# Split GELU product: tiles 2 to 13 taken in pairs of 16 adjacent rows a partition, with joint stores and three rotating buffers

## The chip, the core and the metric

The kernel runs on one core of one Trainium2 chip. The metric is device time in microseconds (us) for one execution, as the median of several runs. A profile is one further execution, recorded by the hardware profiler; its times are counted from the start of its span.

## The reference

The input is `x` of shape 32 x 512 x 2048 in float32, that is 16,384 rows of 2048 values, 134.2 MB. The output has 1024 values for each row, 67.1 MB.

```python
x1, x2 = (x[..., :half_dim].copy(), x[..., half_dim:].copy())
gelu_x1 = 0.5 * x1 * (1 + erf(x1 / np.sqrt(2)))
return (gelu_x1 * x2).astype(np.float32)
```

Each row is read once, its first half goes through GELU, and the result is multiplied by its second half. No value is used twice.

## The kernel before

The rows are cut into 16 tiles of 1024 rows. In a tile, each of the 128 partitions holds R = 8 adjacent rows, so a load brings 64 KB of adjacent bytes to a partition (8.4 MB a tile), and a store writes 32 KB of adjacent bytes from it (4.2 MB a tile).

There are two `x` buffers and two `o` buffers, used by even and odd tiles in turn. A tile goes through four steps. Its load is issued by SyncE (SP) in `load` at L49. ScalarE (ACT) computes GELU from the first half of each row in `x` to `o` at L87, in steps of 5 and 3 rows; tiles 0 and 15 take steps of 2, 2 and 4 rows. VectorE (DVE) multiplies `o` in place by the second half of `x` at L95. A store takes `o` to HBM at L56. ScalarE issues the stores of tiles 0 to 13, and SyncE those of tiles 14 and 15. Tiles 0 and 15 are stored in two halves, tile 0 is also loaded in two halves, and a tiny load on ScalarE's queue comes first.

The order is written out by hand with semaphores. `gelu_done` counts the steps of ScalarE and releases VectorE. `mul_done` counts the multiplications; it releases each store on the queue that issues it, and on SyncE the load of tile i+2, which takes the `x` buffer of tile i. `ready[k]` counts both the loads into `x` buffer k and the stores out of `o` buffer k. ScalarE waits for it before the first step of a tile, so that it waits for the load of tile i and for the store of tile i-2 together:

```python
nc.scalar.wait_ge(ready[k], n[ready[k].name])
...
if i + 2 < n_tiles:
    nc.sync.wait_ge(mul_done, n[mul_done.name])
    load(i + 2, slice(0, R), ready[k])
```

Each engine works through its own instructions in order, waits included. The loads of tiles 0 and 1 are issued ahead of the loop.

Of the kernel before, what the change touches and what calls it, by code (L numbers as in the profile page):

```python
# [1 line left out]

# [4 lines left out]

GELU = mybir.ActivationFunctionType.Gelu


@with_exitstack
def kernel(
    ctx: ExitStack,
    tc: tile.TileContext,
    x: bass.AP,
    out: bass.AP,
):
    nc = tc.nc
    P = nc.NUM_PARTITIONS

    x_flat = x.flatten_outer_dims()
    out_flat = out.flatten_outer_dims()
    n_rows, dim = x_flat.shape
    half = dim // 2

    R = 8
    x_t = x_flat.rearrange("(n p r) d -> n p r d", p=P, r=R)
    o_t = out_flat.rearrange("(n p r) d -> n p r d", p=P, r=R)
    n_tiles = x_t.shape[0]
    x_bufs = [nc.alloc_sbuf_tensor(f"x{k}_tile", [P, R, dim], x.dtype) for k in range(2)]  # L30
    o_bufs = [nc.alloc_sbuf_tensor(f"o{k}_tile", [P, R, half], out.dtype) for k in range(2)]

    first = [nc.alloc_semaphore(f"first{j}") for j in range(2)]
    ready = [nc.alloc_semaphore(f"ready{k}") for k in range(2)]
    gelu_done = nc.alloc_semaphore("gelu_done")
    mul_done = nc.alloc_semaphore("mul_done")
    tail_stored = nc.alloc_semaphore("tail_stored")
    opened = nc.alloc_semaphore("opened")  # L40
    scrap = nc.alloc_sbuf_tensor("scrap_tile", [8, 128], x.dtype)
    n = {sem.name: 0 for sem in [*first, *ready, gelu_done, mul_done, tail_stored, opened]}

    def counted(ins, sem, by):
        ins.then_inc(sem, by)
        n[sem.name] += by

    def load(i, rows, sem):
        ins = nc.sync.dma_start(out=x_bufs[i % 2][:, rows, :], in_=x_t[i][:, rows, :])  # L49
        counted(ins, sem, 16)  # L50
        return ins

    def store(queue, i, rows, sem):
        queue.wait_ge(mul_done, n[mul_done.name])
        counted(
            queue.dma_start(out=o_t[i][:, rows, :], in_=o_bufs[i % 2][:, rows, :]), sem, 16  # L56
        )

    opening = nc.scalar.dma_start(out=scrap[:, :], in_=x_t[0][:8, 0, :128])
    counted(opening, opened, 16)
    for ins in (
        opening,
        load(0, slice(0, 4), first[0]),
        load(0, slice(4, 8), first[1]),
        load(1, slice(0, 8), ready[1]),
    ):  # L70
        tc.no_tile_sem_insts.add(ins.ins.name)
    tc.close()
    tc.compile()  # L73

    for i in range(n_tiles):
        k = i % 2
        last = i == n_tiles - 1
        pieces = i == 0 or last
        steps = ((0, 2), (2, 4), (4, 8)) if pieces else ((0, 5), (5, 8))
        for lo, hi in steps:  # L80
            rows = slice(lo, hi)
            if i == 0 and lo % 4 == 0:
                nc.scalar.wait_ge(first[lo // 4], 16)
            elif lo == 0:
                nc.scalar.wait_ge(ready[k], n[ready[k].name])
            counted(
                nc.scalar.activation(  # L87
                    out=o_bufs[k][:, rows, :], in_=x_bufs[k][:, rows, :half], func=GELU
                ),
                gelu_done,  # L90
                1,
            )
            nc.vector.wait_ge(gelu_done, n[gelu_done.name])
            counted(
                nc.vector.tensor_mul(  # L95
                    out=o_bufs[k][:, rows, :],
                    in0=o_bufs[k][:, rows, :],
                    in1=x_bufs[k][:, rows, half:],
                ),
                mul_done,  # L100
                1,
            )
            if pieces and hi % 4 == 0:
                if last:
                    store(nc.sync, i, slice(hi - 4, hi), tail_stored)
                else:
                    store(nc.scalar, i, slice(hi - 4, hi), ready[k])
        if not pieces:
            if i == n_tiles - 2:
                store(nc.sync, i, slice(0, R), tail_stored)  # L110
            else:
                store(nc.scalar, i, slice(0, R), ready[k])
        if i + 2 < n_tiles:
            nc.sync.wait_ge(mul_done, n[mul_done.name])
            load(i + 2, slice(0, R), ready[k])


    nc.scalar.wait_ge(opened, 16)
    nc.scalar.drain()  # L119
    for sem in (*first, *ready, opened):  # L120
        nc.scalar.sem_clear(sem)
    nc.vector.drain()
    nc.vector.sem_clear(gelu_done)
    nc.sync.sem_clear(mul_done)
    nc.sync.wait_ge(tail_stored, n[tail_stored.name]).then_inc(
        tail_stored, -n[tail_stored.name]
    )


# [1 line left out]
_INS = ['x']  # L131
_OUTS = [((32, 512, 1024), 'float32')]


# [23 lines left out]
```

## Time and profile before

| what | value |
|---|---|
| time, median of 3 runs | 469.36 us (469.31 to 469.44) |
| span of the profiled execution | 467.84 us |
| median time less that span | 1.52 us |
| bytes moved over the span | 201.34 MB, mean 430 GB/s |
| VectorE busy | 140.5 us in 34 instructions |
| ScalarE busy | 115.5 us in 35 instructions |
| loads, issue to landing, median | 44.4 us (15 of the 17) |
| stores of 4 MB on ScalarE's queue, issue to landing, median | 44.7 us |

The span is the time from the first to the last record of the profiled execution. Queue q1 in the profile carries the DMAs that SyncE issues, and queue q10 those that ScalarE issues. Both run on the core's 16 DMA engines. A DMA of 128 partitions is split over all 16 engines, so that each of them moves 8 partitions, in 8 packets. The share of a queue is the time that its packets took, as a part of the time of 16 engines. A name such as `ACTq L56` is a DMA issue on ScalarE's queue at line 56. A "landing" is the moment at which the whole DMA has counted up its semaphore.

### The profile page before, as it was taken

How to read it: one execution, taken by the hardware profiler on the slowest of the kernel's cores; microseconds unless marked ns; L12 is line 12 of the kernel's file. 1: busy time of each engine (PE TensorE's matmuls, PEld its weight loads, DVE VectorE, ACT ScalarE, POOL GpSimd, SP SyncE). 2: the span in 40 equal slices, each digit the busy share in tenths (PEclk: the TensorE clock that was granted, in tenths of full speed). 3: DMA queues.
4: the chain of work that ended last, by engine and by line, in shares of the span. 5: the costliest groups of instructions: out<-in, count | busy, mean ns of one | idle time of the engine just before them, and what ended most of it. 6: DMA issues, size and time to landing. Idle time of an engine off the chain costs nothing.

```text
span 467.8 us, 154 instructions
## 1 busy us (share of the span) xinstructions
DVE 140.5 (30%) x34; ACT 115.5 (25%) x35; POOL 0.2 (0%) x4
## 2 busy tenths in 40 slices
DVE  0330515207051060511606115060150702507043
ACT  1320606041060410604105050050501506014060
POOL 0000000000000000000000000000000000000000
DMA  8999999999999999999999999999999999999988
GB/s 359 448 448 448 398 406 496 403 403 448 459 437 403 440 412 493 403 403 448 487 409 403 445 406 493 403 403 448 493 403 403 448 426 471 403 426 426 493 384 379
DMA packets 5057, 201.34 MB, mean 430 GB/s; under 512 B 568, under 2 KB 576, under 8 KB 576
## 3 DMA queue, kind: packets, MB, share of 16 engines
q1 hardware_dynamic: 2880, 142.61, 70.6%
q10 hardware_dynamic: 2176, 58.73, 29.1%
q14 instruction: 1, 0.01, 0.0%
HBM read 134.22 MB, written 67.11 MB: 430 GB/s over the span
## 4 chain that ended last, share of the span: by engine, by line
DMA 76%; DVE 14%; ACT 8%; ACTq 0%; SPq 0%; issue 0%
DMA out_dram<-o_tile 66%; DVE o_tile L95 14%; DMA x_tile<-in_x_dram 10%; ACT o_tile L87 8%; ACTq L119 0%; SPq L49 0%
## 5 line engine op out<-in xcount | busy, mean ns | idle before, releaser
L95 DVE TENSOR_TENSOR o_tile<-o_tile,x_tile 128x5120 f32<-128x5120 f32 (+3 forms) x34 | 140.5, 4171 | 319.7 <-ACT o_tile L87 319.7
L87 ACT ACTIVATE o_tile<-x_tile 128x5120 f32<-128x5120 f32 (+3 forms) x34 | 114.3, 3407 | 337.3 <-DMA out_dram<-o_tile 301.8
L87 ACT ACT_TABLE_LOAD x1 | 1.3, 1283 | 2.9 <-PEq L73 2.9
L142 POOL MEMSET const-bfloat16-1.0<- 128x1 bf16 x1 | 0.1, 102 | 0.0
L142 POOL MEMSET const-uint8-127<- 128x1 uint8 x1 | 0.1, 101 | 0.0
L142 POOL MEMSET const-float32-0.0<- 128x1 f32 x1 | 0.1, 99 | 0.2 <-issue 0.2
L142 POOL MEMSET const-float32-1.0<- 128x1 f32 x1 | 0.1, 98 | 0.0
## 6 DMA issues: line engine op xcount, KB each, us to landing
out_dram<-o_tile ACTq DMA_DIRECT2D x13, 4096.0 KB, 44.7
x_tile<-in_x_dram SPq DMA_DIRECT2D x2, 4096.0 KB, 16.7
out_dram<-o_tile ACTq DMA_DIRECT2D x2, 2048.0 KB, 34.4
out_dram<-o_tile SPq DMA_DIRECT2D x1, 4096.0 KB, 25.2
out_dram<-o_tile SPq DMA_DIRECT2D x2, 2048.0 KB, 7.8
x_tile<-in_x_dram SPq DMA_DIRECT2D x15, 44.4
scrap_tile<-in_x_dram ACTq DMA_DIRECT2D x1, 4.0 KB
```

The lines of the kernel that those rows point to most:

```text
L87: nc.scalar.activation(out=o_bufs[k][:, rows, :], in_=x_bufs[k][:, rows, :half], func=GELU),
L95: nc.vector.tensor_mul(out=o_bufs[k][:, rows, :], in0=o_bufs[k][:, rows, :], in1=x_bufs[k][:, rows, half:],),
L142: nc = _bacc.Bacc("TRN2", target_bir_lowering=False, num_devices=1)
```

## The change

Tiles 2 to 13 (`PAIRED`) are taken in pairs of an even and an odd tile. In a pair, partition p holds 16 adjacent rows of the 2048-row block: the first 8 belong to the even tile, the other 8 to the odd one. Each tile is still loaded by one DMA with 64 KB of adjacent bytes for each partition, but the partitions are now 128 KB apart in HBM instead of 64 KB.

The `x` and `o` buffers are replaced by three buffers of 64 KB a partition, each of which holds one loaded tile. Odd tiles use buffer 1, and even tiles use buffers 0 and 2 in turn (`buf_of`). GELU now works in place, on the first half of each row. The multiplication writes its products, packed, into the buffer of the even tile: the even tile's products to its lower half, the odd tile's to its upper half (`out_rows`). When the odd tile is multiplied, one store of 64 KB a partition takes both tiles to HBM (`store_pair`, 8.4 MB). Tiles 0, 1, 14 and 15 keep their rows and their separate stores.

The loads of tiles 0, 1 and 2 are issued ahead of the loop. After that, loads are issued at odd tiles only: SyncE waits for the multiplication of tile i, issues the load of tile i+2 into buffer 1, then waits for the store of the pair to land, and issues the load of tile i+3 into the buffer from which that store has read. VectorE waits for its own previous multiplication before each new one. The instructions of ScalarE and VectorE keep their number and the elements they work on. The stores of tiles 2 to 13 are six DMAs instead of twelve.

```diff
-    x_bufs = [nc.alloc_sbuf_tensor(f"x{k}_tile", [P, R, dim], x.dtype) for k in range(2)]
-    o_bufs = [nc.alloc_sbuf_tensor(f"o{k}_tile", [P, R, half], out.dtype) for k in range(2)]
+    n_tiles = n_rows // (P * R)
+    PAIRED = range(2, n_tiles - 2)
 
+    def rows_of(flat, i):
+        if i in PAIRED:
+            first = (i - i % 2) * P * R
+            block = flat[first : first + 2 * P * R, :]
+            return block.rearrange("(p r) d -> p r d", p=P)[:, (i % 2) * R : (i % 2 + 1) * R, :]
+        return flat[i * P * R : (i + 1) * P * R, :].rearrange("(p r) d -> p r d", p=P)
 
+    bufs = [nc.alloc_sbuf_tensor(f"m{k}_tile", [P, 2 * R, half], x.dtype) for k in range(3)]
+
+    def buf_of(i):
+        return 1 if i % 2 else i % 4
+
+    def x_rows(i, lo, hi, part):
+        pairs = bufs[buf_of(i)][:, 2 * lo : 2 * hi, :].rearrange("p (r two) d -> p r two d", two=2)
+        return pairs[:, :, part, :]
+
+    def out_rows(i, lo, hi):
+        at = (i % 2) * R
+        return bufs[buf_of(i - i % 2)][:, at + lo : at + hi, :]
...
-    def load(i, rows, sem):
-        ins = nc.sync.dma_start(out=x_bufs[i % 2][:, rows, :], in_=x_t[i][:, rows, :])
+    def load(i, lo, hi, sem):
+        pairs = bufs[buf_of(i)][:, 2 * lo : 2 * hi, :].rearrange("p (r two) d -> p r (two d)", two=2)
+        ins = nc.sync.dma_start(out=pairs, in_=rows_of(x_flat, i)[:, lo:hi, :])
...
+    def store_pair(queue, i, sem):
+        queue.wait_ge(mul_done, n[mul_done.name])
+        base = (i - 1) * P * R
+        both = out_flat[base : base + 2 * P * R, :].rearrange("(p r) d -> p r d", p=P)
+        counted(queue.dma_start(out=both, in_=bufs[buf_of(i - 1)][:, :, :]), sem, 16)
...
-        load(0, slice(0, 4), first[0]),
-        load(0, slice(4, 8), first[1]),
-        load(1, slice(0, 8), ready[1]),
+        load(0, 0, 4, first[0]),
+        load(0, 4, 8, first[1]),
+        load(1, 0, 8, ready[1]),
+        load(2, 0, 8, ready[2]),
...
-                nc.scalar.activation(
-                    out=o_bufs[k][:, rows, :], in_=x_bufs[k][:, rows, :half], func=GELU
-                ),
+                nc.scalar.activation(out=x_rows(i, lo, hi, 0), in_=x_rows(i, lo, hi, 0), func=GELU),
...
+            if n[mul_done.name]:
+                nc.vector.wait_ge(mul_done, n[mul_done.name])
             nc.vector.wait_ge(gelu_done, n[gelu_done.name])
             counted(
                 nc.vector.tensor_mul(
-                    out=o_bufs[k][:, rows, :],
-                    in0=o_bufs[k][:, rows, :],
-                    in1=x_bufs[k][:, rows, half:],
+                    out=out_rows(i, lo, hi),
+                    in0=x_rows(i, lo, hi, 0),
+                    in1=x_rows(i, lo, hi, 1),
                 ),
...
-        if not pieces:
-            if i == n_tiles - 2:
-                store(nc.sync, i, slice(0, R), tail_stored)
-            else:
-                store(nc.scalar, i, slice(0, R), ready[k])
-        if i + 2 < n_tiles:
+        if i == n_tiles - 2:
+            store(nc.sync, i, 0, R, tail_stored)
+        elif i == 1:
+            store(nc.scalar, i, 0, R, ready[0])
+        elif i % 2 and i in PAIRED:
+            store_pair(nc.scalar, i, ready[buf_of(i - 1)] if i + 3 < n_tiles else tail_stored)
+        if i % 2 and i + 2 < n_tiles:
             nc.sync.wait_ge(mul_done, n[mul_done.name])
-            load(i + 2, slice(0, R), ready[k])
-
+            load(i + 2, 0, R, ready[1])
+            if i + 3 < n_tiles:
+                a = buf_of(i + 3)
+                nc.sync.wait_ge(ready[a], n[ready[a].name])
+                load(i + 3, 0, R, ready[a])
```

More of the change, by code (lines that the diff above doesn't have):

```diff
@@ L46, in counted, with store @@
         n[sem.name] += by
-    def load(i, rows, sem):
-        ins = nc.sync.dma_start(out=x_bufs[i % 2][:, rows, :], in_=x_t[i][:, rows, :])
+    def load(i, lo, hi, sem):
+        pairs = bufs[buf_of(i)][:, 2 * lo : 2 * hi, :].rearrange("p (r two) d -> p r (two d)", two=2)
+        ins = nc.sync.dma_start(out=pairs, in_=rows_of(x_flat, i)[:, lo:hi, :])
         counted(ins, sem, 16)
         return ins
-    def store(queue, i, rows, sem):
+    def store(queue, i, lo, hi, sem):
         queue.wait_ge(mul_done, n[mul_done.name])
         counted(
-            queue.dma_start(out=o_t[i][:, rows, :], in_=o_bufs[i % 2][:, rows, :]), sem, 16
-        )
-    opening = nc.scalar.dma_start(out=scrap[:, :], in_=x_t[0][:8, 0, :128])
+            queue.dma_start(out=rows_of(out_flat, i)[:, lo:hi, :], in_=out_rows(i, lo, hi)),
+            sem,
+            16,
+        )
+    def store_pair(queue, i, sem):
[3 more added lines that the diff above has]
+        counted(queue.dma_start(out=both, in_=bufs[buf_of(i - 1)][:, :, :]), sem, 16)
+    opening = nc.scalar.dma_start(out=scrap[:, :], in_=x_flat[:8, :128])
     counted(opening, opened, 16)
@@ L75 @@
     for i in range(n_tiles):
-        k = i % 2
+        k = buf_of(i)
         last = i == n_tiles - 1
@@ L80 @@
         for lo, hi in steps:
-            rows = slice(lo, hi)
             if i == 0 and lo % 4 == 0:
```

9 lines of the change are left out of this document (3 added, 6 removed).

## Prediction, made before the changed kernel was run

> **What bounds the kernel now.** I read the page first, then stretches with their DMA share, then the chain of waits, then DMA traffic in short windows, and last the trace's records of single DMA packets, which lie under these views.
>
> The page's busy times and DMA queues:
>
> ```profile
> DVE 140.5 (30%) x34; ACT 115.5 (25%) x35; POOL 0.2 (0%) x4
> ...
> q1 hardware_dynamic: 2880, 142.61, 70.6%
> q10 hardware_dynamic: 2176, 58.73, 29.1%
> ```
>
> No compute engine is busy a third of the time; the two DMA queues (q1 SyncE's, q10 ScalarE's) together fill 99.7% of 16 engines' span. Stretches of two tiles show it as share (next to last column) and GB/s:
>
> ```profile
> 100.00:158.00 58.00, 17.52 (x4) 14.25 (x4) 0.00 (x0) 1.00 1.00 434
> 158.00:216.00 58.00, 17.52 (x4) 14.24 (x4) 0.00 (x0) 1.00 1.00 434
> ```
>
> The DMA engines never rest here: two tiles move 25.17 MB in 58.0 us. The chain (start, us, what) says the same from the compute side:
>
> ```profile
> 60.31 40.07 DMA out_dram<-o_tile
> 100.38 0.02 issue
> 100.40 4.48 ACT o_tile L87
> 104.88 0.02 issue
> 104.91 8.77 DVE o_tile L95 x2
> ```
>
> Compute waits for a landing and takes 13.3 us from it (100.40 to 113.68). In the packet records a 64 KB packet takes 2.418 us, a 32 KB one 1.213, a 16 KB one 0.611, a semaphore entry 0.009; the values hardly vary. Every DMA puts 8 packets and one semaphore entry on each engine, and packets follow each other without a gap from 1.74 us to 467.4 us. Where both queues hold work, an engine takes one packet from each in turn: a tile costs 8 x (2.418 + 1.213) = 29.05 us, and tiles do come every 29.0 us. So the time is bytes on the DMA engines. An edit can save only packet overhead, and loses whatever time it leaves these engines empty.
>
> **The change, part by part.** The sum is made on the profiled execution: span 467.84 us, to which 1.52 us around it lead up to the median 469.36.
>
> *Larger stores.* On each engine 96 packets of 1.213 become 48 of 2.418: 116.45 - 116.06 = 0.38 us, and six DMAs fewer are six semaphore entries, 0.05. Gain 0.44 us.
>
> The Trainium skill ("DMA: Bandwidth & Descriptors", Anatomy of one DMA) gives each DMA about 2 us of fixed cost beside its bytes. By it six DMAs fewer would save 12 us; the trace disagrees, because packets of other DMAs already fill that time.
>
> *Compute.* Shapes and counts of L87 and L95 stay. VectorE now also waits for its own previous multiplication. Queued behind that wait is only the next multiplication, and ScalarE's store waits for both anyway. Bound: from 0 to 0.1 us a tile (the chain's steps show 0.02 us handovers); I take 0, hidden as long as packets cover it.
>
> *Loads, the part that decides.* Before, each of SyncE's loads needs only the multiplication of tile i (x and product have buffers of their own), so q1 always holds about 15 us of work: a load lands 44.4 us after its issue while one takes 29. After, the even tile's buffer also holds both products, so load i+3 waits on SyncE for the store of the pair. Queued behind this wait is the next odd load, which needs the next pair's multiplication, 58 us later, and loses nothing. But at the moment of that wait q1 holds only the odd load. There are six such turns: loads 4, 6, 8, 10, 12, 14.
>
> *Turn 1* can be read off the trace of before, since all up to there is the same. Tile 1 is multiplied at 60.31, store 1 and load 3 go out together and alternate. DMA traffic from 96 to 104 us in 40 slices of 0.2 us, a packet counted where it starts:
>
> ```profile
> GB/s 1966 328 0 0 0 0 0 0 0 0 0 1311 1147 164 0 0 0 1966 2949 328 0 0 0 0 0 0 0 0 0 819 1475 328 0 0 0 983 3604 655 0 0
> ```
>
> The burst at 96.0 is load 3's last packet, at 98.3 store 1's last, and at 99.5 come both semaphore entries and the first packet of the next load, already queued. After the change that packet is not queued. Its issue must wait for the store's landing: 100.38 in the chain. From the first load's issue at 0.73 to first packets at 1.74 to 2.29 (mean 1.86) are 1.13 us, so engines start at 100.40 + 1.13 = 101.53. They ended at 99.51 to 99.84, mean 99.68: 1.85 us empty. First packets after emptiness are slower: the kernel's first 16 took 1.64 to 2.06, mean 1.80, against 1.21, so 0.59 more. Turn 1 costs 2.44 us (1.85 if the slow start is the kernel's start alone).
>
> *Turns 2 to 6* are empty too unless the pair store is ahead of the odd load, so that a load packet (2.42 us) lies behind the store's semaphore entry: it must cover the spread between engines (0.34, from the records), the entry's way to its landing (99.85 to 100.38, 0.53), the wake (0.02) and the issue (1.01), together 1.90. So: where does a new store enter a busy engine? One row shows it, the first store. Issue and queue traffic in the 5 us behind it:
>
> ```profile
> 19.26 0.38 ACTq L56 DMA_DIRECT2D out_dram<-o_tile  x1
> ```
> ```profile
> DMA packets 64, 2.10 MB, mean 411 GB/s; under 512 B 16, under 2 KB 16, under 8 KB 16
> ...
> q1 hardware_dynamic: 64, 2.10, 100.0%
> ```
>
> The whole answer from 19.2 to 24.3 us holds no q10 row. With the idle delay of 1.01 the store reaches the engines at 20.27, when all still run the seventh 32 KB packet. The eighth, the semaphore entry and a 64 KB packet go first; the store's packets start at 24.36. So three entries seem committed ahead. Now turn 2: load 3 lands 0.3 us before store 1 (44.4 against 44.7 on the page), at 100.10; tile 3 is multiplied at 100.12 + 13.27 = 113.39; the pair store reaches the engines at 113.39 + 1.13 = 114.5. Load 4 started at 101.53; with the slow start its sixth packet runs from 114.2 to 116.6. Committed: seventh, eighth, semaphore. Then store and load 5 alternate from their first packets, both semaphores come last, and the engines run empty again. Later turns repeat it; there the store's data ends a packet earlier, so its receipt may be 0.26 us shorter (the load's 0.3 lead): 2.2 us. Six turns: 2.44 + 5 x 2.2 = 13.4 us. Bounds: without slow starts 1.85 + 5 x 1.6 = 9.9; all at the first price 14.6. I take 13.4, the rows as they stand.
>
> *Ends.* The tail keeps its order: load 15, store 14, two pieces; store 14 is queued before load 15 ends, and the last piece, 11.7 + 1.1 us behind load 15's landing, still comes within the 14.6 us that store 14 and the first piece fill. Load 2 issued at the start stands behind load 1 either way. Both 0.
>
> Sum: 467.84 + 1.52 - 0.44 + 13.4 = 482.3, forecast 482 us.
>
> **Rivals.**
> *Every other turn is covered.* If only two entries are committed (the first store's issue then took over 1.2 us under load), the store of turn 2 slips in before load 4's semaphore and stays one packet ahead: 2.42 covers 1.90. The next load then starts earlier, its store finds only the eighth packet and the semaphore, and that turn is empty. Three turns: 2.44 + 2 x 2.2 - 0.44 = +6.4, 475.8 us. For it: 114.5 lies only 0.3 us inside the sixth packet.
>
> *Only turn 1 is empty*, if new stores enter at the next packet: 2.44 - 0.44 = +2.0, 471.4 us (470.8 without a slow start). Against it: the first store missed two packet boundaries.
>
> *Not slower: every landing is covered.* If at each load 4, 6 to 14 a packet of the odd load still lies behind the store's semaphore, nothing is empty and 0.44 us are gained: 468.9 us. It decides from cover above 1.90 us; for it stands the 2.42 us packet, against it the burst at 99.5, where both entries come together. This is also the case in which the change's waits do not do what I read.
>
> *Slower reading.* Paired loads step 128 KB between partitions instead of 64. If their packets take longer, 96 of them on each engine carry it: each 1% of 2.418 is 2.3 us. Rows bound it only far off: from 0 (no load packet after the first differs with its address) to 0.59 a packet, 57 us. I take 0 and give it a small chance, on top of the forecast above 485.
>
> The Trainium skill ("DMA: Bandwidth & Descriptors", Latency and other measured facts) speaks against the change here: copies lose rate at large power-of-two row pitches, 207 GB/s at 512 KiB against 214 for a padded one. Were that 3.3% to hold at 128 KB, 7.6 us would be added, 490 us; no run here shows it, and 64 KB shows no loss.
>
> **How the numbers follow.** A measurement of this kernel tells about 0.2% (0.94 us) from no change. Forecast (six empty turns) 0.45, every other 0.25, turn 1 alone 0.13, none 0.07, slower reading or longer empty turns 0.10. Slower holds all but the fourth and a little of the third case: 0.90; same 0.07; faster 0.03, as 0.44 us is under the bound. Range: from 470.8 (turn 1 alone, low price) to 485 (all turns at the first price, and 1 us for longer receipts). Left out: none empty, and reading slower.
>
> **What would show it.** After: span near 481; DMA share per 60 us below 0.98 with gaps of some 1.7 us, about every 60 us, the first at 99.5 to 101.5; SyncE's loads waiting for stores; no q10 packet in the last third of a pair's period. Load packets above 2.42 us would show slow reading. Share 1.00 at 101 us would break the step on turn 1; gaps there and at every second turn, the step on three committed entries.

## The result, and the profile after

The changed kernel takes 484.16 us (483.47 and 484.84 in two executions) against 469.39 us before: ratio 1.0315, 95% interval 1.0296 to 1.0335, slower. The forecast was 482.0, with a range of 470.8 to 485.0. Two more of its executions, four of six with the odd load in two DMAs (one of them the traced one) and three of six of the changed kernel again were 1.7 to 5.5% above the shortest of the same kernel; the times and ratios here leave them out, and nothing on record says why they are longer. The span of the profiled execution grew from 467.84 to 483.4 us, by 15.6 us.

The page's busy times and DMA queues of the changed kernel:

```profile
DVE 141.9 (29%) x34; ACT 115.5 (24%) x35; POOL 0.2 (0%) x4
...
q1 hardware_dynamic: 2880, 142.61, 70.4%
q10 hardware_dynamic: 1312, 58.72, 28.1%
```

The bytes are the same, and q10 has 864 packets fewer, as it should. The shares alone split the loss. Before, 99.7% of 467.84 us were 466.4 us of packets on each engine; now 98.5% of 483.4 are 476.1. So packets themselves take 9.7 us more, and the engines stand empty for 5.9 us more. Of the first kind the prediction had only the slow first packets, 6 x 0.59 = 3.5 us; the rest of its loss was empty time.

Stretches of 60 us (next to last column the DMA share, last the GB/s):

```profile
100.00:160.00 60.00, 17.70 (x4) 14.24 (x4) 0.00 (x0) 1.00 1.00 419
160.00:220.00 60.00, 17.70 (x4) 14.25 (x4) 0.00 (x0) 1.00 0.97 419
220.00:280.00 60.00, 17.70 (x4) 14.24 (x4) 0.00 (x0) 1.00 1.00 421
...
340.00:400.00 60.00, 17.70 (x4) 14.24 (x4) 0.00 (x0) 1.00 1.00 418
```

Before, share 1.00 went with 434 GB/s. A share of 1.00 at 418 means busy engines whose packets are slow: a busy share alone would have hidden this. (A packet is counted whole in the stretch where it starts, so a share can be off by some hundredths; the first stretch holds the emptiness of turn 1 and still shows 1.00.)

SyncE's waits (in total, times, longest) show the new wait of the loads for stores. The kernel before has the first of these lines, the changed kernel the other two:

```profile
SPq L49 <- DVE o_tile L95: 396.5, 14, 29.4
```
```profile
SPq L65 <- DMA out_dram<-m_tile: 257.0, 6, 44.0
SPq L65 <- DVE m_tile L115: 152.3, 7, 57.2
```

Turn 1 in DMA traffic, 96 to 104 us in slices of 0.2 us, the window that the prediction showed of before:

```profile
GB/s 2949 983 0 0 0 0 0 0 0 0 0 655 1475 492 0 0 0 0 0 0 0 0 0 0 0 0 0 3932 655 655 0 0 0 0 0 0 0 0 0 0
```

After store 1's last packets, which start from 98.2 to 98.8, no data packet starts until 101.4. In the packet records the engines are empty for 1.84 us on the mean; the prediction had 1.85.

The even loads after turn 1 (99 to 124 us, slices of 0.625 us) and after turn 2 (157 to 184 us, slices of 0.675 us). Each cluster is the start of one round of 16 packets:

```profile
GB/s 0 0 0 734 944 0 0 0 839 839 0 0 1258 419 0 0 1258 419 0 0 1573 105 0 0 1573 105 0 0 1678 0 0 0 0 524 1153 0 0 944 734 0
```
```profile
GB/s 97 0 1068 485 0 0 1456 97 0 777 680 97 0 1456 97 0 97 1359 97 0 1262 291 0 0 1456 97 0 874 680 0 0 1456 97 0 583 874 97 0 1262 291
```

In the first, rounds follow every four slices (2.5 us), with two exceptions: the first round, and the one before the last two clusters. The records give load 4's first packets 3.10 us and its seventh 3.61 us, against 2.42; the seventh is the one directly ahead of the pair store's first packet. In the second line rounds stay regular: turn 2 was covered, nothing was empty, and neither slow packet appears.

Over the six turns (a turn is a place where an even load waits for a store to land) the records of this execution give, in us on the mean engine:

| turn, even load | empty | first packet over 2.42 | last load packet(s) ahead of the store, over 2.42 |
|---|---|---|---|
| 1, load 4 | 1.84 | 0.68 | 1.21 |
| 2, load 6 | 0 | 0 | 0 |
| 3, load 8 | 1.00 | 0.70 | 1.06 |
| 4, load 10 | 0.10 | 0.48 | 1.55 |
| 5, load 12 | 0.27 | 0.81 | 1.11 |
| 6, load 14 | 0.88 | 0.63 | 1.38 |
| sum | 4.1 | 3.3 | 6.3 |

At the end, engines finish 1.6 us apart instead of 0.45, and the tail is empty for 1.6 us more. With 0.5 us of other slow load packets and the 0.44 gained this is 15.4 of 15.6 us.

### The profile page after: what moved, and what is told of

It is laid out like the page before. It is cut to its first block, busy times and chain, and to the rows that moved or that the text cites. A ratio compares the mean times of both kernels' runs of the same rounds, so it can differ in the third digit from the quotient of the medians.

```text
span 483.4 us, 182 instructions
## 1 busy us (share of the span) xinstructions
DVE 141.9 (29%) x34; ACT 115.5 (24%) x35; POOL 0.2 (0%) x4
## 4 chain that ended last, share of the span: by engine, by line
DMA 76%; DVE 14%; ACT 8%; ACTq 0%; issue 0%; SPq 0%; DVEq 0%
DMA m_tile<-in_x_dram 76%; DVE m_tile L115 14%; ACT m_tile L107 8%; ACTq L143 0%; SPq L65 0%; DVEq L113 0%
## 5 line engine op out<-in xcount | busy, mean ns | idle before, releaser
L115 DVE TENSOR_TENSOR m_tile<-m_tile 128x5120 f32<-128x5120 f32 (+3 forms) x34 | 141.9, 4174 | 333.8 <-ACT m_tile L107 333.2
L107 ACT ACTIVATE m_tile<-m_tile 128x5120 f32<-128x5120 f32 (+3 forms) x34 | 114.3, 3407 | 352.2 <-DMA m_tile<-in_x_dram 352.2
```

The source lines that it names most:

```text
L107: nc.scalar.activation(out=x_rows(i, lo, hi, 0), in_=x_rows(i, lo, hi, 0), func=GELU),
L115: nc.vector.tensor_mul(out=out_rows(i, lo, hi), in0=x_rows(i, lo, hi, 0), in1=x_rows(i, lo, hi, 1),),
```

## The experiments

Theory 1: the loss is the engines left empty at the turns, and the restart. Theory 2: paired loads read slowly because their partitions lie 128 KB apart. After the first four runs came theory 3: beside emptiness, the change from a run of loads to a store costs time. Ratios are to the kernel before, run beside, at 469.25 to 469.30 us.

**The map of rows alone**, in the kernel before:

```diff
-        ins = nc.sync.dma_start(out=x_bufs[i % 2][:, rows, :], in_=x_t[i][:, rows, :])
+        ins = nc.sync.dma_start(out=x_bufs[i % 2][:, rows, :], in_=rows_of(x_flat, i)[:, rows, :])
```

(and `rows_of(out_flat, i)` in the store)

> The kernel before with the paired map of rows alone: its own four buffers, its own order and its own stores of 32 KB a partition; loads step 128 KB between partitions and stores 64 KB. Theory 1: nothing is left empty, 469.4 us (469.2 to 469.6). Theory 2: the paired loads' packets are slow here too, up to 10 us: 472 to 479 us.

Measured 469.25 us, ratio 1.0000 (0.9991 to 1.0008). Its page has the queue shares of before, digit for digit:

```profile
q1 hardware_dynamic: 2880, 142.61, 70.6%
q10 hardware_dynamic: 2176, 58.73, 29.1%
```

Theory 2 falls: from tile 2 on its load packets take 2.418 us. The Trainium skill ("DMA: Bandwidth & Descriptors", Latency and other measured facts) reports losses at row pitches from 512 KiB; here, at 128 KB with 64 KB pieces, there is none.

**The store ahead of the odd load, in SyncE's queue:**

```diff
-            store(nc.scalar, i, 0, R, ready[0])
+            store(nc.sync, i, 0, R, ready[0])
-            store_pair(nc.scalar, i, ...
+            store_pair(nc.sync, i, ...
```

> Only the queue of the joint stores (and of store 1) changes: SyncE issues the store ahead of load i+2, so that both stand in one queue and the whole odd load lies behind the store. Theory 1 (the loss is engines left empty at the six turns, and the restart after them): every turn is covered by 19 us of load, DMA share 1.00 throughout, and the 0.44 us of the larger stores remain: 468.9 us (468.6 to 469.3). Theory 2 (packets of the paired loads are slow because partitions lie 128 KB apart): slow load packets stay, 84 ns a packet above 2.42 us on the mean, 10 us in all: about 479 us.

Measured 472.39 us, ratio 1.0064 (1.0052 to 1.0076): four fifths of the loss are gone by covering the turns, with the map of rows, the buffers and the joint stores unchanged. But 468.9 was missed by 3.5 us. Two stretches of it:

```profile
160.00:220.00 60.00, 17.70 (x4) 15.38 (x5) 0.00 (x0) 1.00 1.01 436
...
450.00:467.00 17.00, 9.01 (x3) 7.22 (x3) 0.00 (x0) 1.00 0.86 366
```

The middle runs at full rate; the tail does not. The kernel before has in the same stretch:

```profile
450.00:467.00 17.00, 8.92 (x3) 5.72 (x3) 0.00 (x0) 1.00 1.00 428
```

The tail's DMA traffic from 442 to 472 us, slices of 0.75 us:

```profile
GB/s 0 961 437 0 786 437 175 0 481 350 437 524 218 568 393 393 524 437 393 524 218 87 44 44 328 677 371 350 350 481 240 655 371 371 350 459 568 22 44 0
```

Between 457.8 and 460.3 us most engines are empty (1.79 us on the mean). In the records one engine starts its last 64 KB packet of load 15 at 449.9, when the others are done with theirs or nearly so. The load has landed only when the last engine has, tile 15 is computed that much later, and its stores come after the other engines have run dry. What drove the engines apart is in the records too: the last load packets ahead of a store take 0 to 0.45 us longer on the mean and up to 1.2 us longer on single engines.

**The odd load in two DMAs:**

```diff
-            load(i + 2, 0, R, ready[1])
+            load(i + 2, 0, 4, ready[1])
+            load(i + 2, 4, 8, ready[1])
```

> The changed kernel with each odd load issued as two DMAs of 32 KB a partition, so that it has 16 packets on an engine against the store's 8. Theory 1 with turns taken by packets: the store ends while 8 load packets (9.7 us) are still queued, all six turns are covered, and 8 ns for each of 56 more packets an engine cancel the gain: 469.4 us (469.0 to 470.5). If engines shared by bytes, store and load would end together as before: about 484 us. Theory 2 (128 KB between partitions): about 479 us.

Measured 472.2 and 472.6 us, ratio 1.0066 (1.0049 to 1.0083), 1.9 us above the range. Twice as many load packets on the same bytes cover the turns, as turns taken by packets demand; sharing by bytes (484) falls. The only trace of this form is not of these executions; in it no engine is empty between the start and 235 us, which takes in turns 1 to 3. Where the remaining 3 us lie is not shown.

**Two stores a pair:**

```diff
-        elif i % 2 and i in PAIRED:
-            store_pair(nc.scalar, i, ready[buf_of(i - 1)] if i + 3 < n_tiles else tail_stored)
+        elif i in PAIRED:
+            pair = i - i % 2
+            store(nc.scalar, i, 0, R, ready[buf_of(pair)] if pair + 4 < n_tiles else tail_stored)
```

> The changed kernel with its three in-place buffers and its map of rows, but each tile of a pair is stored by a DMA of its own as soon as it is multiplied. The even buffer is still loaded only after the odd tile's store has landed. Theory 1: at that landing the even store of the next pair stands in ScalarE's queue, the engines are never empty, 469.4 us (469.2 to 470.5). Theory 2: about 479 us. If the wait for the landing itself were the cost, whatever is queued beside it: about 484 us.

Measured 471.09 us, ratio 1.0038 (1.0025 to 1.0051), 0.6 us above the range. The load still waits for the last store's landing, so the wait itself is not the cost. Turn 1 is (96 to 112 us, slices of 0.4 us):

```profile
GB/s 655 0 0 0 0 983 328 0 983 328 0 901 410 0 737 573 0 655 655 0 655 246 819 655 328 492 164 164 0 246 164 0 819 328 328 901 0 655 492 0
```

Store 2's packets fill the engines from 99.5, and load 4, issued at 100.3, enters behind them at 104.8; its first two packets take 3.50 and 2.95 us. After that hardly a load packet differs from 2.418. The engines are empty for only 0.25 us on the mean here. So the slow packets do not need empty engines: it was enough that the loads had paused for some 5 us, with none queued.

**The same with turn 1 covered**, load 3 alone being split:

```diff
-            load(i + 2, 0, R, ready[1])
+            if i == 1:
+                load(i + 2, 0, 4, ready[1])
+                load(i + 2, 4, 8, ready[1])
+            else:
+                load(i + 2, 0, R, ready[1])
```

> The form with two stores a pair, with load 3 alone split into two DMAs, so that at turn 1 (load 4) 8 packets of 32 KB of load 3 are still queued when store 1 ends. Theories 1 and 3: that form lost 1.8 us at turn 1 and nothing later, where the two queues alternate without a break; now turn 1 is covered: 469.4 us (469.2 to 469.8). If its loss lies elsewhere: 471.1 us as without the split.

Measured 470.33 us, ratio 1.0023 (1.0013 to 1.0032): 0.8 us of the 1.8 came back. From 60 us on no group of load packets is slow by more than 0.2 us any more; the engines finish 1.36 us apart. The forecast of 469.4 (469.2 to 469.8) was missed: the traced execution has 0.6 us more of empty engines than the kernel before, nearly all of it in that spread at the end, and 0.7 us more of packets.

**The store behind the odd load:** SyncE issues load i+2 first, then the store, then waits for its landing.

```diff
-        elif i == 1:
-            store(nc.scalar, i, 0, R, ready[0])
-        elif i % 2 and i in PAIRED:
-            store_pair(nc.scalar, i, ...
...
             load(i + 2, 0, R, ready[1])
+            if i == 1:
+                store(nc.sync, i, 0, R, ready[0])
+            else:
+                store_pair(nc.sync, i, ...
```

> The joint stores (and store 1) go to SyncE's queue behind load i+2, not ahead of it. The store is then the last thing in the queue at all six turns, and the even load is issued after its landing. Theory 1: six full turns of 1.85 us empty and 0.6 us of slow first packets: 468.9 + 6 x 2.45 = 483.6 us. Theory 3: these six and 0.1 to 1.2 us more at each change from loads to a store: 484 to 491 us. If emptiness cost nothing and only the changes of direction did: 472 us, as with the store ahead of the load.

Measured 491.78 us, ratio 1.0478 (1.0464 to 1.0491). Its stretches and one turn (157 to 187 us, slices of 0.75 us):

```profile
160.00:220.00 60.00, 17.70 (x4) 14.24 (x4) 0.00 (x0) 1.00 0.95 402
```
```profile
GB/s 0 0 1311 87 0 0 0 0 1311 87 0 0 1398 0 0 1311 87 0 961 437 0 262 1136 0 87 1311 0 0 1311 87 0 1136 262 0 699 699 0 87 1311 0
```

The four zeros are store 3's last packet and the emptiness behind it. All six turns are alike in the records: 1.90 us empty on the mean (1.76 to 2.25), first packets 0.67 us slow, and the last load packet ahead of the store 1.10 us slow, the sixteenth packet after the restart. A full turn costs 3.67 us; six on the 468.9 of a covered kernel are 490.9. Measured is 0.8 us above theory 3's range, 484 to 491; theory 1's 483.6 lacks the third term, the slow last packet.

**The kernel before with all stores in SyncE's queue:** `store(nc.scalar, ...)` becomes `store(nc.sync, ...)` for tiles 0 to 13.

> The kernel before with its stores of tiles 0 to 13 on SyncE's queue instead of ScalarE's: nothing of the change is in it, q1 always holds about 14 us of work, and each engine now moves 8 load packets in a run and then 8 store packets in a run. Theory 1 (only emptiness and restart cost): 469.3 us (469.1 to 469.7). Theory 3 (beside emptiness, the change from a run of loads to a store costs: the last load packet takes 0.1 to 1.2 us longer, not alike on the engines): 14 such changes at the 0.1 to 0.4 us seen in the one-queue form of the changed kernel: 471 to 475 us.

Measured 474.36 us, ratio 1.0112 (1.0098 to 1.0127), inside theory 3's range and far from theory 1's 469.3. Nothing waits anew and no buffer is shared:

```profile
q1 hardware_dynamic: 5040, 201.33, 99.3%
```

Before each store the last load packet is slow: 1.34 us at the first store, which follows the kernel's start, and 0 to 0.4 us later, 2.4 us in all. The tail then loses another 2.0 us to engines that are out of step. The range was thus met partly by terms that theory 3 did not have: its price at each change, without the first store, makes little more than 1 us. The Trainium skill ("DMA: Bandwidth & Descriptors", Issuing engines are not separate DMA queues) says that issuing from several engines saves only the sequencer's time. Here the measurement differs: the second queue is worth 5.1 us. With it loads and stores alternate packet by packet; in one queue they come in runs of eight.

**The kernel before with each load in two DMAs:**

```diff
-            load(i + 2, slice(0, R), ready[k])
+            load(i + 2, slice(0, 4), ready[k])
+            load(i + 2, slice(4, 8), ready[k])
```

> The kernel before with each load of tiles 2 to 15 issued as two DMAs of 32 KB a partition: 16 load packets an engine stand against a store's 8, so that ScalarE's queue runs dry for about 10 us of every 29 while SyncE's stays full; nothing of the change is in it. Theory 1: nothing is empty, 8 ns for each of 112 more packets an engine: 470.3 us (469.8 to 470.6). Theory 3 with its price in unbroken streams: 14 stores begin behind a run of loads, 0.1 to 0.4 us each: 471.5 to 476 us. If that price is paid only in one queue or after a restart: 470.3 us as well.

Eleven runs fall into two groups, 470.1 to 470.4 (five) and 473.4 to 474.5 (six); ratio 1.0058 (1.0036 to 1.0081). The lower group lies at theory 1's 470.3. The trace is of the upper one, and its DMA traffic from 442 us on (slices of 0.78 us) shows the same kind of hole as with the store ahead of the load:

```profile
GB/s 420 378 546 336 378 546 336 420 588 294 462 504 294 546 420 336 588 378 336 588 252 42 42 42 315 483 504 357 336 483 210 599 378 357 357 630 336 63 21 0
```

The engines are empty for 2.08 us there and finish 1.6 us apart, while slow packets make only about 1 us. So in an unbroken stream the change of direction itself is cheap, and what costs is that engines come out of step. That they stay in step in the lower group is an inference; no trace of it was taken.

**The changed kernel again:**

> The changed kernel once more, on the chip of these runs and with more rounds: 482 to 486 us in its undisturbed runs. The trace should again show turn 1 empty for 1.8 us, the first packets of even loads slow by 0.6 to 0.8 us where their turn was empty, and the last load packet ahead of each joint store slow by about 1.1 us.

Measured 484.4, 488.2 and 489.8 us, ratio 1.0386 (1.0350 to 1.0423), above the range in two of three. The trace is of the execution of 489.8. Turn 1 repeats to within 0.1 us: 1.91 empty, 0.66 and 1.18 slow. The later turns do not: turn 2 was covered again, and the others were empty for 0.17, 0.87, 0.20 and 6.67 us. The slow packet ahead of the store shows at all turns but the second, by 1.2 to 1.4 us. Turn 6 is the costly one. A stretch of 50 us around it, and its DMA traffic from 396 to 412 us (slices of 0.4 us):

```profile
400.00:450.00 50.00, 17.11 (x4) 14.24 (x4) 0.00 (x0) 1.00 0.87 362
```
```profile
GB/s 0 0 819 655 819 328 0 0 492 164 164 164 0 0 0 164 0 0 0 164 0 0 0 0 0 0 0 0 0 1966 492 164 0 0 0 0 819 1638 164 0
```

Ten engines had finished the store's packets by 398.2 us, three more by 399.5, the last three at 402.8, 404.5 and 406.1. The load could be issued only after the last, its packets start at 407.6, and the engines were empty for 6.67 us on the mean.

No version beat the kernel before; its map of rows alone equals it.

## Why the prediction was right, and where it was not

*What bounds the kernel, and what the change can gain:* right. With its turns covered, the changed kernel comes close to the time of before. The joint stores' packets do take 2.418 us, but no form shows the 0.44 us as a gain. The 2 us for each DMA that the prediction takes from the Trainium skill ("DMA: Bandwidth & Descriptors", Anatomy of one DMA) are fitted there to DMAs issued by GpSimd. Here fourteen more DMAs of SyncE, the split loads, cost 1.0 us in the lower group of runs, under 0.1 us each.

*Turn 1:* right in each term: 1.85 us forecast and 1.84 and 1.91 found empty, 0.59 forecast and 0.66 to 0.68 found for the first packets. Two of its means are a little off, though: in the records the first packets start at 1.90 on the mean, not 1.86, and the engines end at 99.65, not 99.68, which would have made 1.92 of the 1.85.

*"So three entries seem committed ahead":* wrong, and this was the step that made all six turns empty. By the delay of 1.13 us that the prediction uses, the pair store reached the engines at 114.9, in load 4's sixth packet; only the seventh went ahead of it, and it started at 120.16. In load 6 it came in the seventh and only the eighth passed. The three entries came from one sample, the first store, read with the delay of 1.01 us measured at the idle start; with a longer delay under load the same row shows fewer. As the rival "every other turn" has it, turn 2 was covered (two packets), but later turns fell between: 1.00, 0.10, 0.27 and 0.88 us empty.

*The spread of 0.34 us between engines:* wrong after turn 1. It grew to 0.8 us at turn 2 and to one engine 1.7 us late at turn 3, and a landing waits for the last engine. Later turns spread further, up to 2.5 us between the first and the last engine to finish the store. With it the calculated cover of single packets lost its meaning.

*The sum:* the empty time was put at 9.9 us and was 4.1. Missing were a term of 6.3 us, the last load packet ahead of the store, and 1.6 us of the tail, which the prediction had put at 0. What was too much and what was missing nearly cancel, so 482 was close to 484 partly by chance; the repeated kernel, up to 489.8, went past the range; the store behind the load, where all six turns are empty as forecast, shows what that step would really have cost: 491.8.

*Slow reading by address:* rightly given a small chance, and excluded by the map of rows alone. Its sign was badly chosen: load packets above 2.42 us did appear, from another cause. The sign for the main case, a DMA share below 0.98 about every 60 us, showed in only one of six stretches, since slow packets filled the time.

*Compute:* a multiplication pair takes 8.87 instead of 8.77 us, and from a landing to the issue of the store a tile takes 13.48 us (100.31 to 113.79) instead of 13.30 (100.40 to 113.70). These 0.18 us are above the bound of 0.1 that was given. They do not enter the sum: at the turns SyncE waits for a landing, and between them packets fill the time.

## What to carry to other kernels

On a kernel that fills its DMA engines, ask of every wait ahead of a load what else stands in the queues at that moment, counted in packets; a store's landing that the next load waits for needs more cover than landing, wake and issue, because the slowest engine sets it. Read GB/s beside the busy share, since packets can slow down with the share at 1.00. Two queues that held the same number of packets kept the engines in step here; a change that breaks this pairing has to be priced even where nothing waits.

## What had not been expected of the hardware

Loads that restart when their queue has run out pay twice. With the store behind the load it is 0.67 us at the first packet, and 1.10 us at the last packet before the next store, the sixteenth after the restart (the seventh at turn 1 of the changed kernel); in an unbroken stream that second price is 0 to 0.45 us. Empty engines are not needed for the first price: it is 0.48 and 0.81 us at turns 4 and 5 of the changed kernel, where they were empty for under 0.3 us on the mean. A run of stores between loads is not enough: in one queue, eight store packets ahead of loads that are already queued left the first load packet at 2.42 us. Why both prices depend on the restart is open.

The 16 engines run in step (0.33 to 0.45 us from first to last) through the whole kernel before, and drift apart as soon as loads and stores no longer alternate one by one: by up to 5.1 us in the changed kernel, 8.2 in the kernel before with split loads, and 9.1 at turn 6 of the repeated run. What makes single engines fall behind, beyond the slow packets seen, stays open as well.
